# A whole transformer layer on one core: tiles with written places, new step tables for its first half, and a last product in two halves

## The chip, the cores and the metric

The kernel runs on one core of a Trainium2 chip. Its engines are TensorE (PE, which multiplies matrices), VectorE (DVE), ScalarE (ACT), GpSimd (POOL), and SyncE (SP), whose queue issues most transfers. The metric is the device time of one execution in microseconds, the median of several runs; less is better.

## The reference

One layer of a diffusion backbone is computed in float32, for 128 context tokens and 128 latent tokens of 2048 channels, with the same weights for both groups:

```python
m = silu(c) @ w_ada + b_ada                       # shift1, scale1, gate1, shift2, scale2, gate2
h = rms_norm(x) * (1 + scale1) + shift1
p = h @ w_in                                      # [q_A k_A v_A | q_B k_B v_B | gate_A gate_B]
o_A = windowed attention(q_A, k_A, v_A)           # 8 heads of 128, 2 key heads
o_B = neighbourhood attention(q_B, k_B, v_B)      # 8 heads of 128
merged = (sigmoid(gate_A) * (o_A @ w_br_a) + sigmoid(gate_B) * (o_B @ w_br_b)) @ w_out
x = x + gate1 * merged
h2 = rms_norm(x) * (1 + scale2) + shift2
y = x + gate2 * (relu(h2 @ w_up) ** 2 @ w_down)   # 2048 -> 8192 -> 2048
```

The new keys and values of both mixers are outputs too.

## The kernel before, in words

**Products.** Each float32 operand is split in two parts of a shorter form: `hi` is a copy in the shorter type, `lo` is the value less `hi`. A product is then three matmuls: hi by hi, hi by lo, lo by hi. The tokens stand in two blocks of 128 (context and latent), and the weights stream through as the moving operand.

**Steps.** All weight products are a list of steps, `wsteps`. One step is one weight tile `raw` of 128 rows by 1024 values (512 KB): two slices of 512 columns, two token blocks, three matmuls each, so twelve matmuls of 512 columns into two PSUM banks `acc`. The tile is loaded by SP's queue, copied to `wH` by ACT (line 103), and subtracted to `wL` by DVE (line 281). For the steps in `LO_DMA`, the low half is made by an accumulating transfer that POOL issues (lines 287 and 288) and DVE does nothing.

**What sets the order.** The order is written out; the engines each follow their own queue in that order. `run()` (line 305) goes through the steps. Ahead of a step's products it issues all loads up to `RUN[i]` steps ahead and prepares the tiles up to `LOOK[i] + 1` steps ahead; behind the products it runs what the calendar `cal[i]` holds for that step, entered there with `at(i, fn)`. So the strings `RUN` and `LOOK` and lists of step numbers (`DOTS`, `POST`, `JOBS`, `ADA_AT`, `XS_AT`, `SS_AT`) fix where each piece of small work stands in each engine's queue. A step of products that no one holds up takes 2.72 us, twelve times 0.227.

**Buffers.** All large tiles (`raw`, `wH`, `wL`, `araw`, `u_...`, `xnT` and so on) come from `G()`, which takes the next of 50 places of 4 KB per partition in rotation, the pool `gen`.

**The opening and the first 224 steps.** `begin()` (line 575 on) writes the steps 0 to 2 out by hand. The input projection follows in five chunks of channels (2, 2, 2, 4 and 6 tiles of 128). Each chunk needs its modulated input, for which the modulation (shift and scale) of two channel tiles at a time is made by `mod_pair(f)` (line 540): eight loads `araw` of 512 KB, sixteen column-tiled matmuls (line 366, 32 rows of the trace) into one bank `ps_ada`, a copy `S` by ACT, four transposes by PE into `ps_sel` (line 380), a sum by DVE, then the modulated and split input. `ADA_AT[f]` is the step at which it stands, and the transposes stand one step later. `SS_AT` does the same for the second sub-layer in two halves of eight matmuls. A unit of the projection that continues a sum from an earlier chunk either seeds its banks with ACT copies (`SEED1` has a 1) or adds by DVE behind its products (a 0, line 476).

The gates of the residuals are computed on DVE as dot products (line 1499, two instructions of 128 by 1024 each), placed by `DOTS`. The attention stands in steps 80 to 130: norms and rotation (`POST`), and for eight jobs of heads the scores (line 861), softmax, transposes to `ps_PT` (line 911), their copy `probT` by ACT, and the weighted values (lines 918 and 922), placed by `JOBS`. After it come the two branch products, the output product, the up and the down products.

**The ending.** `last_unit` (line 1216) does the last 512 output columns. The last two weight tiles' products for the latent tokens come last; then DVE multiplies by the gate and adds (lines 1067 and 1069) in two halves of 256 columns, each followed by its store (line 1411).

## Time and profile before

| | before |
|---|---|
| time, median of 3 runs (us) | 1313.86 (1313.8 to 1314.27) |
| time of the profiled execution (us) | 1313.68 |
| its span, first to last instruction (us) | 1311.8 |
| PE busy (us, share) | 1298.4, 99% |
| DVE busy | 1146.1, 87% |
| ACT busy | 917.5, 70% |
| POOL busy | 58.5, 4% |
| granted clock of TensorE, mean | 1.00 |
| HBM read, written (MB) | 373.97, 8.70 |

The span is less than the time by 1.9 us, which lie around the first and last instruction. A row of the timeline begins with the start and the duration in microseconds; in brackets behind it stands how long the engine had idled before and on what. Matmuls overlap: two neighbours start 0.227 us apart, though each is shown with 0.39 us, so waits of PE are read from the distances of starts.

### The profile page before, as it was taken

The page shows a single profiled execution, that of the slowest core. Times are in us where ns is not written, and L with a number is a line of the kernel's source. Part 1 is how long each engine was busy: PE and PEld are TensorE (multiplying, and loading weights), DVE is VectorE, ACT ScalarE, POOL GpSimd, SP SyncE. Part 2 cuts the span into 40 slices and gives each one's busy share as a digit, 9 for nine tenths or more (in the row PEclk, how much of TensorE's full clock was granted, in tenths as well). Part 3 has the DMA queues.
Part 4 walks back from the last instruction along what each step waited for, and adds up shares of the span by engine and source line. Part 5 has one row for each costly group of instructions (what it writes and reads, how often), then busy time and mean ns, then how long its engine had stood idle before and what let it go on. Part 6 is the DMA issues. An engine that isn't in the chain of part 4 may idle for free.

```text
span 1311.8 us, 17435 instructions
## 1 busy us (share of the span) xinstructions
PE 1298.4 (99%) x5978; PEld 1052.2 (80%) x5978; DVE 1146.1 (87%) x1532; ACT 917.5 (70%) x1289; POOL 58.5 (4%) x67
## 2 busy tenths in 40 slices
PE   8999999999999999999999999999999999999998
PEld 4767888888777778888888888888888888888886
DVE  4578999999899999999879998897989999979653
ACT  5657766689765657645687857869678787796881
POOL 0000000341100000000000000000000000000000
PEclk9999999999999999999999999999999999999999
DMA  9999998897889999999399775788586696968692
GB/s 379 418 411 420 361 365 320 306 364 278 290 347 365 419 384 330 369 344 372 113 321 317 244 256 179 273 293 282 201 297 224 212 317 248 297 161 304 204 345 78
DMA packets 148313, 393.80 MB, mean 300 GB/s; under 512 B 51680, under 2 KB 52672, under 8 KB 148224
## 3 DMA queue, kind: packets, MB, share of 16 engines
q1 hardware_dynamic: 144064, 378.18, 77.7%
q0 software_dynamic: 4016, 14.42, 5.7%
q8 instruction: 47, 0.77, 0.2%
q14 instruction: 42, 0.34, 0.1%
q10 hardware_dynamic: 144, 0.08, 0.0%
HBM read 373.97 MB, written 8.70 MB: 292 GB/s over the span
## 4 chain that ended last, share of the span: by engine, by line
PE 70%; DVE 3%; ACT 0%; issue 0%; DVEq 0%; ACTq 0%
PE acc L332 14%; PE acc L333 14%; PE acc L334 14%; PE Q L1281 6%; PE Q L1283 6%; PE Q L1282 6%; PE Z L1281 1%; PE Z L1283 1%; PE Z L1282 1%; DVE aT L1499 1%; DVE junk L1499 1%; PE acc L1119 1%; PE acc L1120 1%; PE acc L1102 1%; PE acc L1101 1%; PE acc L1103 1%
## 5 line engine op out<-in xcount | busy, mean ns | idle before, releaser
L281 DVE TENSOR_TENSOR wL<-raw,wH 128x1024 fp32r<-128x1024 f32 x361 | 425.7, 1224 | 62.4 <-ACT wH L103 61.8
L103 ACT ACTIVATE wH<-raw 128x1024 fp32r<-128x1024 f32 (+1 forms) x391 | 387.4, 1043 | 49.7 <-PE acc L334 10.2
L1499 DVE SCALAR_TENSOR_TENSOR aT<-aT,cB 128x1024 f32<-128x1024 f32 x144 | 173.9, 1224 | 1.1
L1499 DVE SCALAR_TENSOR_TENSOR junk<-aT,cB 128x1024 bf16<-128x1024 f32 x144 | 173.9, 1224 | 0.0
L463 PE MATMUL acc<-wH,hH 128*128 128x512 f32 x276 | 108.2, 392 | 0.0
L465 PE MATMUL acc<-wH,hL 128*128 128x512 f32 x276 | 107.5, 389 | 0.0
L464 PE MATMUL acc<-wL,hH 128*128 128x512 f32 x276 | 107.5, 389 | 0.0
L103 ACT ACTIVATE uH<-raw 128x1024 fp32r<-128x1024 f32 x34 | 36.1, 1063 | 65.7 <-DVE raw L1345 57.9
L463 PEld LDWEIGHTS acc<-wH,hH 128*128 128x128 f32 x276 | 51.8, 188 | 13.8 <-issue 2.5
L465 PEld LDWEIGHTS acc<-wH,hL 128*128 128x128 f32 x276 | 51.8, 188 | 10.9
L464 PEld LDWEIGHTS acc<-wL,hH 128*128 128x128 f32 x276 | 51.8, 188 | 10.6
L103 ACT ACTIVATE tH<-t 128x1024 fp32r<-128x1024 f32 x34 | 36.0, 1058 | 28.7 <-DVE t L1338 26.5
L332 PE MATMUL acc<-wH,hH 128*128 128x512 f32 x128 | 52.6, 411 | 0.0
L333 PE MATMUL acc<-wL,hH 128*128 128x512 f32 x128 | 50.1, 392 | 1.3 <-DVE wL L281 1.3
L498 PE MATMUL acc<-wH,hH 128*128 128x512 f32 x128 | 50.5, 394 | 0.0
L499 PE MATMUL acc<-wL,hH 128*128 128x512 f32 x128 | 49.9, 390 | 0.1
L334 PE MATMUL acc<-wH,hL 128*128 128x512 f32 x128 | 50.1, 391 | 0.0
L500 PE MATMUL acc<-wH,hL 128*128 128x512 f32 x128 | 50.0, 390 | 0.0
L1348 DVE TENSOR_TENSOR uL<-raw,uH 128x1024 fp32r<-128x1024 f32 x34 | 41.7, 1226 | 1.4 <-ACT uH L103 0.3
L103 ACT ACTIVATE acc<-dsum 128x512 f32<-128x512 f32 x56 | 31.7, 590 | 15.7 <-DVE t L1067 8.3
L1338 DVE TENSOR_TENSOR t<-raw 128x1024 f32<-128x1024 f32 x34 | 41.4, 1219 | 1.3 <-PE Q L1282 1.3
L1347 DVE TENSOR_TENSOR tL<-t,tH 128x1024 fp32r<-128x1024 f32 x34 | 41.4, 1219 | 0.0
(652 smaller groups left out, 3331.9 us busy)
## 6 DMA issues: line engine op xcount, KB each, us to landing
raw<-in_w_in SPq DMA_DIRECT2D x133, 512.0 KB, 7.6
raw<-in_w_down SPq DMA_DIRECT2D x128, 512.0 KB, 6.3
aT<-in_w_adaT SPq DMA_DIRECT2D x80, 512.0 KB, 8.0
raw<-in_w_upF SPq DMA_DIRECT2D x68, 512.0 KB, 5.4
aT<-in_w_gT SPq DMA_DIRECT2D x64, 512.0 KB, 7.7
raw<-in_w_up SPq DMA_DIRECT2D x60, 512.0 KB, 6.2
araw<-in_w_pair SPq DMA_DIRECT2D x48, 512.0 KB, 8.9
raw<-in_w_out SPq DMA_DIRECT2D x32, 512.0 KB, 9.2
```

The source lines that it names most:

```text
L103: act.activation(out, in_, AF.Copy)
L281: dve.tensor_tensor(st["lo"], st["raw"], st["hi"].bitcast(F32), op=OP.subtract)
L332: pe.matmul(acc[tb], sh, wh[:, k, :], start=f, stop=False, skip_group_check=seeded)
L333: pe.matmul(acc[tb], sh, wl[:, k, :], start=False, stop=False, skip_group_check=seeded)
L334: pe.matmul(acc[tb], sl, wh[:, k, :], start=False, stop=l, skip_group_check=seeded)
L463: pe.matmul(acc[tb], sh, wh[:, k, :], start=opened[u] and k == 0, stop=False, skip_group_check=skip)
L464: pe.matmul(acc[tb], sh, wl[:, k, :], start=False, stop=False, skip_group_check=skip)
L465: pe.matmul(acc[tb], sl, wh[:, k, :], start=False, stop=last and k == 1, skip_group_check=skip)
L1281: pe.matmul(acc, stat[0], hi, start=f, stop=False)
L1282: pe.matmul(acc, stat[0], lo, start=False, stop=False)
L1283: pe.matmul(acc, stat[1], hi, start=False, stop=l)
L1499: dve.scalar_tensor_tensor(out, box["raw"], 1.0, cB[s, tag], op0=OP.mult, op1=OP.mult, accum_out=dst[:, s, fb:fb + 1])
```

## The change

**Places written down.** `G()` no longer rotates. A string `SLOTS` gives for every tile, in the order in which they are asked for, the letter of one of 53 places, each a buffer of its own. Three more tiles are 12 KB more per partition; the program is built with a space of 4096 bytes for DMA descriptors (`SCRATCH`), which it did not set before.

**New tables.** For the first 224 steps `LOOK`, `RUN` (digits now to base 36, the largest 14 where it was 9), `LO_DMA`, `DOTS1`, `DOTS`, `SEED1` (25 ones where there were 27), `POST`, `JOBS`, `XS_AT` and `M_AT` are other numbers; `DOTS2` and the digits of the later steps stay.

**The modulation in four pieces.** `wide_load` and `wide_mm` now handle two `araw` tiles (four matmuls) at a time, and `ADA[f]` gives for each of the four pieces the step of its loads and of its products, then the steps of the transposes, of the input and of its split. `SS` does so for the second sub-layer.

**Warm-up.** The tile `wr`, its two copies by ACT, and the six matmuls on it in `begin()` are replaced by six matmuls of the other warm-up form.

**The ending.** The last 24 products become 48 of 256 columns by the words of the change; in the program built from it, twelve matmuls of 512 columns become twenty-four of 256 (each with its weight load), first all of the left half, then the DVE work of that half, then the right half.

```diff
@@ -28,13 +28,15 @@
-GEN = 50
+SLOTS = 'ABCDEFGHIJKLMNOPQRSTUVWXYZabcdefghijklmnopqrstuvwxyz0GHIJKLMNERSTUOPhdQiVekjWXYaZbmlpocuvsrwyzTSAPOx0IWjJKYXNZ...
+GEN = 53
+SCRATCH = 4096
...
-SEED1 = "111110100100111111011111111001011111"
+SEED1 = "010010101101111110101110011111111110"
...
-LO_DMA = [50, 54, 56, 63, 77, 107, 129, 144, 145, 176, 184, 188, 189, 203, 228, 233, 250, 286, 297, 360, 388, 392, 403, 447]
+LO_DMA = [50, 54, 57, 63, 77, 107, 118, 126, 132, 142, 144, 184, 188, 189, 203, 233, 250, 286, 297, 360, 388, 392, 403, 447]
...
-ADA_AT = [None, 4, 13, 22, 25]
-XS_AT = {1: 3, 2: 24, 3: 34}
...
-JOBS = [[93, 94, 95, 100, 106], [93, 94, 99, 104, 106], [98, 98, 100, 105, 114], [101, 104, 107, 110, 111], [107, 107, 110, 115, 118], [109, 109, 111, 118, 121], [113, 114, 115, 126, 128], [116, 116, 119, 122, 124]]
-SS_AT = [118, 127]
+ADA = {1: [[1, 2, 3, 5], [0, 2, 4, 5], [5, 5, 5]], 2: [[13, 14, 15, 18], [11, 14, 16, 17], [18, 19, 20]], 3: [[17, 18, 18, 22], [17, 18, 21, 21], [21, 21, 27]], 4: [[24, 26, 26, 26], [25, 27, 27, 27], [28, 29, 30]]}
+XS_AT = {1: 1, 2: 19, 3: 20}
...
+JOBS = [[92, 94, 99, 102, 106], [94, 95, 100, 104, 106], [98, 99, 100, 106, 114], [103, 104, 108, 110, 111], [107, 107, 110, 114, 119], [108, 109, 111, 119, 122], [114, 114, 115, 123, 126], [114, 116, 119, 123, 124]]
+SS = [[[117, 119, 122, 126], [116, 119, 125, 127], 129]]
...
@@ -90,8 +92,13 @@
+    slots = iter(SLOTS)
+
+    def slot():
+        return {"tag": "g" + next(slots), "bufs": 1} if SLOTS else {"tag": "g"}
+
     def G(name, dt=F32):
-        return gp.tile([P, 1024], dt, name=name, tag="g")
+        return gp.tile([P, 1024], dt, name=name, **slot())
...
-    wr = G("wr", F32R)
...
-    for h in range(2):
-        copy(wr[:, 512 * h:512 * h + 512], wm)
...
-    def wide_load(box, nsub, f, half):
-
-        for q in range(4 * half, 4 * half + 4):
+    def wide_load(box, nsub, f, j):
+
+        for q in (2 * j, 2 * j + 1):
...
     def mod_pair(f):
 
         box, k0 = {}, 2 * f
-        i = ADA_AT[f]
-        for j in range(2):
-            load_at(i, lambda j=j: wide_load(box, 0, f, j))
-            at(i, lambda j=j: wide_mm(box, j))
-        at(i, lambda: ada_evac(box))
-        at(i + 1, lambda: ada_cols(box, 0, k0, 2))
-        at(i + 2, lambda: make_h(k0, 2))
-        at(i + 3, lambda: split_h(k0, 2))
+        come, go, (c, m, s) = ADA[f]
+        for j in range(4):
+            load_at(come[j], lambda j=j: wide_load(box, 0, f, j))
+            at(go[j], lambda j=j: wide_mm(box, j))
+        at(go[3], lambda: ada_evac(box))
+        at(c, lambda: ada_cols(box, 0, k0, 2))
+        at(m, lambda: make_h(k0, 2))
+        at(s, lambda: split_h(k0, 2))
...
-        warm_r(*[(P, wr[:, 0:512])] * 3, *[(P, wr[:, 8:520])] * 3)
+        warm(6)
...
-        def mms(q, tb):
+        def mms(q, tb, c=slice(0, 512)):
             wh, wl = box["hl"][q]
+            acc = box["acc"][tb][:, c]
             for k in range(2):
                 sh, sl = stat(q // 2)(2 * (q % 2) + k, tb)
...
+                pe.matmul(acc, sh, wh[:, k, c], start=False, stop=False, skip_group_check=True)
+                pe.matmul(acc, sh, wl[:, k, c], start=False, stop=False, skip_group_check=True)
+                pe.matmul(acc, sl, wh[:, k, c], start=False, stop=q == n - 1 and k == 1, skip_group_check=True)
...
                     evac_s(box["acc"], 0)
-                    mms(q - 1, 1)
-                    mms(q, 1)
                     for c in (slice(0, 256), slice(256, 512)):
+                        mms(q - 1, 1, c)
+                        mms(q, 1, c)
                         evac_s(box["acc"], 1, c)
...
-    nc = bacc.Bacc("TRN2", target_bir_lowering=False, num_devices=1)
+    nc = bacc.Bacc("TRN2", target_bir_lowering=False, num_devices=1, dynamic_dma_scratch_size=SCRATCH)
```

On SP, behind the opening, where the first pair's modulation is loaded (`raw` are weight tiles, `araw` the modulation's), before:

```order
L255 DMA raw_182<-in_w_in 128x1024 [waits DMAHW3_49]
L255 DMA raw_184<-in_w_in 128x1024 [waits DMAHW4_49]
L255 DMA raw_186<-in_w_in 128x1024 [waits DMAHW5_49]
L255 DMA raw_188<-in_w_in 128x1024 [waits DMAHW6_49]
L196 DMA silu_151<-srow_224 32x128 [waits DMAHW7_49,Activation_49]
L255 DMA raw_366<-in_w_in 128x1024 [waits DMAHW0_49]
L356 DMA araw_372<-in_w_pair2 128x1024 [waits DMAHW1_49]
L356 DMA araw_374<-in_w_pair2 128x1024 [waits DMAHW2_49]
L356 DMA araw_376<-in_w_pair2 128x1024 [waits DMAHW3_49]
```

and of the change:

```order
L253 DMA raw_179<-in_w_in 128x1024 [waits DMAHW3_49]
L253 DMA raw_181<-in_w_in 128x1024 [waits DMAHW4_49]
L354 DMA araw_183<-in_w_pair2 128x1024 [waits DMAHW5_49]
L354 DMA araw_185<-in_w_pair2 128x1024 [waits DMAHW6_49]
L253 DMA raw_187<-in_w_in 128x1024 [waits DMAHW7_49]
L354 DMA araw_189<-in_w_pair2 128x1024 [waits DMAHW0_49]
L354 DMA araw_191<-in_w_pair2 128x1024 [waits DMAHW1_49]
L253 DMA raw_193<-in_w_in 128x1024 [waits DMAHW2_49]
L194 DMA silu_148<-srow_229 32x128 [waits DMAHW3_49,Activation_49]
L354 DMA araw_371<-in_w_pair2 128x1024 [waits DMAHW4_49]
```

The first four modulation tiles have moved ahead: two stand in front of the third weight tile, two in front of the fourth, and the rest comes two by two behind that.

On PE, where the transposes `ps_sel` of the first pair's modulation stand, before:

```order
L464 MATMUL acc_465<-wL_357,hH0_248 128x512
L465 MATMUL acc_465<-wH_355,hL0_249 128x512
L380 MATMUL ps_sel_481<-ident_93,S_454 128x128 [waits Activation_49]
L380 MATMUL ps_sel_481<-ident_93,S_454 128x128 x3
L463 MATMUL acc_491<-wH_368,hH0_248 128x512
L464 MATMUL acc_491<-wL_370,hH0_248 128x512 [waits DVE_49]
```

and of the change:

```order
L364 MATMUL ps_ada_401<-araw_379,rt_90 32x512 [waits DMAHW0_49]
L364 MATMUL ps_ada_401<-araw_379,rt_90 32x512
L364 MATMUL ps_ada_401<-araw_381,rt_90 32x512 [waits DMAHW1_49]
L364 MATMUL ps_ada_401<-araw_381,rt_90 32x512
L378 MATMUL ps_sel_482<-ident_92,S_480 128x128 [waits Activation_49]
L378 MATMUL ps_sel_482<-ident_92,S_480 128x128 x3
L461 MATMUL acc_498<-wH_430,hH0_253 128x512
```

Before, the transposes stand between products, twelve of them behind the last modulation matmul; now they follow the last piece's matmuls at once, and ACT's copy `S` of that same bank is what they wait for.

On PE at the very end, before (`acc_11557` is the latent tokens' bank):

```order
L1225 MATMUL acc_11557<-wL_11582,a15H_11336 128x512
L1226 MATMUL acc_11557<-wH_11580,a15L_11337 128x512
L1224 MATMUL acc_11557<-wH_11580,a15H_11336 128x512
L1225 MATMUL acc_11557<-wL_11582,a15H_11336 128x512
L1226 MATMUL acc_11557<-wH_11580,a15L_11337 128x512
```

and of the change, around the place where the left half ends and the right half begins:

```order
L1225 MATMUL acc_11548<-wH_11571,a15L_11328 128x256
L1223 MATMUL acc_11548<-wH_11571,a15H_11327 128x256
L1224 MATMUL acc_11548<-wL_11573,a15H_11327 128x256
L1225 MATMUL acc_11548<-wH_11571,a15L_11328 128x256
L1223 MATMUL acc_11548<-wH_11567,a15H_11327 128x256 [waits DVE_49]
L1224 MATMUL acc_11548<-wL_11569,a15H_11327 128x256
L1225 MATMUL acc_11548<-wH_11567,a15L_11328 128x256
```

The products have half the columns and twice the number, and the right half's first one waits for a DVE instruction, the multiplication that reads the left half of the same bank; the program before has no wait among its last twelve.

## What was predicted

> **What bounds the kernel now.** I read the busy line of the page first, then windows of 20 us, then the timeline of TensorE (PE) in each window with idle time. The columns of a window are its stretch, its length, then busy time and number of instructions of PE, weight load, VectorE (DVE), ScalarE (ACT), GpSimd, then the granted clock, the DMA share and GB/s.
>
> ```profile
> PE 1298.4 (99%) x5978; PEld 1052.2 (80%) x5978; DVE 1146.1 (87%) x1532; ACT 917.5 (70%) x1289; POOL 58.5 (4%) x67
> 60.00:80.00 20.00, 19.87 (x105) 13.81 (x104) 11.05 (x19) 12.72 (x20) 0.00 (x0) 1.00 1.03 417
> 320.00:340.00 20.00, 19.10 (x103) 15.80 (x101) 19.83 (x37) 19.22 (x65) 6.23 (x6) 1.00 0.84 284
> 400.00:420.00 20.00, 19.24 (x106) 16.25 (x105) 20.00 (x33) 12.49 (x18) 0.86 (x1) 1.00 0.98 353
> ```
>
> PE is busy 1298.4 of 1311.8 us and the clock is full, so a schedule can win only what is left in PE's pauses: 13.4 us, a good part of it in the opening and the ending. The tables that change govern the first 224 steps. The pauses there that I can name are these (start, duration, and in brackets the idle time with its releaser):
>
> ```profile
> 75.80 0.39 PE L498 MATMUL acc<-wH,hH 128*128 128x512 f32 x1
> 76.32 0.50 PE L499 MATMUL acc<-wL,hH 128*128 128x512 f32 x1
> 334.41 0.48 PE L332 MATMUL acc<-wH,hH 128*128 128x512 f32 x1
> 335.45 0.50 PE L333 MATMUL acc<-wL,hH 128*128 128x512 f32 x1 [0.56 <-DVE wL L281]
> 367.11 0.39 PE L334 MATMUL acc<-wH,hL 128*128 128x512 f32 x1
> 368.72 0.70 PE L918 MATMUL ps_o<-probT,u_kvA 128*128 128x512 f32 x1 [1.22 <-ACT probT L103]
> 413.92 0.39 PE L332 MATMUL acc<-wH,hH 128*128 128x512 f32 x1
> 415.07 0.50 PE L333 MATMUL acc<-wL,hH 128*128 128x512 f32 x1 [0.76 <-DVE wL L281]
> 473.43 0.27 PE L1520 MATMUL ps_gr<-ident,gc_g 128*32 128x128 f32 x1 [0.82 <-DVE gc_g L1505]
> ```
>
> Products of 512 columns normally start 0.227 us apart (1306.41 and 1306.64 in the last fence below). By starts, the low half wL comes late by 76.32 - 75.80 - 0.227 = 0.3 us, by 0.8 and by 0.9, with some 0.1 more each on the next interval: 2.3 us in three places. The softmax weights probT come late by 1.61 - 0.227 = 1.4 us. The gate rows gc_g come late by 0.8. Added to them is the opening's modulation load:
>
> ```profile
> 29.51 0.39 PE L463 MATMUL acc<-wH,hH 128*128 128x512 f32 x1
> 35.04 3.45 PE L366 MATMUL ps_ada<-araw,rt 128*32 128x512 f32 x24
> 38.68 1.05 PE L366 MATMUL ps_ada<-araw,rt 128*32 128x512 f32 x4 [0.19 <-DMA araw<-in_w_pair]
> 39.98 1.05 PE L366 MATMUL ps_ada<-araw,rt 128*32 128x512 f32 x4 [0.25 <-DMA araw<-in_w_pair]
> 40.97 0.50 PE L463 MATMUL acc<-wH,hH 128*128 128x512 f32 x1
> 41.08 0.60 ACT L103 ACTIVATE S<-ps_ada 128x512 f32<-128x512 f32 x1 [5.33 <-PE ps_ada L366]
> 41.58 2.00 ACT L103 ACTIVATE wH<-raw 128x1024 fp32r<-128x1024 f32 x2
> DMA packets 3467, 11.69 MB, mean 417 GB/s; under 512 B 398, under 2 KB 430, under 8 KB 3466
> ```
>
> The last line is the DMA view of 20 to 48 us: 0.524 MB at 417 GB/s is 1.26 us per tile, and the last two of the eight modulation tiles reach PE 1.30 us apart. From 35.04 to 40.97 PE needs 5.9 us for a block that elsewhere takes 3.6 (next fence): it waits 2.3 us.
>
> **The wide pieces.** The modulation's blocks of column-tiled products are cut in four and laid between ordinary products. By PE's order 6 blocks become 15 (some pieces stand together). What does another block cost?
>
> ```profile
> 65.84 0.39 PE L465 MATMUL acc<-wH,hL 128*128 128x512 f32 x1
> 66.16 3.64 PE L366 MATMUL ps_ada<-araw,rt 128*32 128x512 f32 x32
> 69.73 0.50 PE L463 MATMUL acc<-wH,hH 128*128 128x512 f32 x1
> 70.07 0.40 PE L464 MATMUL acc<-wL,hH 128*128 128x512 f32 x1
> 393.51 0.39 PE L334 MATMUL acc<-wH,hL 128*128 128x512 f32 x1
> 393.83 1.92 PE L366 MATMUL ps_ada<-araw,rt 128*32 128x512 f32 x16
> 395.68 1.05 PE L922 MATMUL ps_o<-probT,u_vB 128*128 128x128 f32 x7
> ```
>
> A whole block of 32 records takes 69.73 - 65.84 - 0.227 = 3.66 us, a half of 16 takes 395.68 - 393.51 - 0.227 = 1.94. Two halves are 0.22 dearer than one whole, and the return costs 70.07 - 69.73 - 0.227 = 0.11 more: 0.33 us a block. Nine more are **+3.0**. Nothing hides this: it is PE's own time. The attention's short groups (scores, transposes, values) stand side by side more often, about seven returns fewer at 0.08 each (rows in the last fence: 353.95 - 353.64 - 0.227): **-0.6**. The bounds are +2.0 to +3.0; I take +2.4.
>
> **The first block's wait.** In the new order of SP's queue the first two pieces' tiles come after raw tiles 3 and 4, the second pair behind raw 5; before, all eight came behind raw 7. With tile eight at 39.95 and 1.26 a tile, the slots are 24.9, 26.2, 27.4, 28.7, 29.9, 31.2, 32.4. PE reaches the pieces at 29.51. The first two tiles are there (27.4, 28.7) and take 0.9; tile three comes at 31.2 and tile four at 32.4: waits of 0.75 + 0.85 = 1.6 us for 2.3 before: **-0.7**. The later pieces' tiles land at least 1.5 us ahead. If PE waited for nothing it would be -2.3.
>
> **Transposes that follow their copy at once.** For pairs 1 and 3 the four transposes of S now stand right behind the last piece on PE; before, a step of twelve products lay between. ACT started the copy 0.11 after PE's next product (41.08 against 40.97) and took 0.60; with the hand-off PE stands 0.75 us: twice, **+1.5**. ACT had idled 5.33 us before that copy, so I take it as prompt; behind two copies of wH it would be 2.0 us more each.
>
> **The stalls the tables move.** The first three (wL) lie in places where DVE's queue runs short. Added over its rows, DVE has by the products of the second stall 9.9 us less work ahead than before, for the dot products of the gate vectors are placed earlier, into the first 100 us, where DVE is busy 11.05 of 20. I take them away: **-2.3**; kept, 0. Two more units than before begin without a seed, which costs DVE four additions:
>
> ```profile
> L476 DVE TENSOR_TENSOR u_qA<-u_qA,acc 128x512 f32<-128x512 f32 x4 | 2.7, 688 | 4.1 <-PE acc L465 4.0
> L1499 DVE SCALAR_TENSOR_TENSOR aT<-aT,cB 128x1024 f32<-128x1024 f32 x144 | 173.9, 1224 | 1.1
> L281 DVE TENSOR_TENSOR wL<-raw,wH 128x1024 fp32r<-128x1024 f32 x361 | 425.7, 1224 | 62.4 <-ACT wH L103 61.8
> ```
>
> That is 4 x 0.69 = 2.8 us, in the second chunk, under cover of the same idle time; without cover it is +2.8. The row of L1499 is one half of a dot product, that of L281 the subtraction that makes a wL. Between job 5's scores and its weighted values lie 24 products now and 12 before, 2.7 us for a stall of 1.4: **-1.4**. The chain to gc_g keeps its shape: 0. The warm-up products and the copies that fed them lie ahead of a wait for hH: 0. The new places and the smaller descriptor space move no instruction by themselves: 0, and a load that waited for its place would cost PE what it is late.
>
> **The ending.** The last twelve products become 24 of 256 columns. The rows are those of the scores, 128 columns each, and of the kernel's last microseconds:
>
> ```profile
> L861 PEld LDWEIGHTS ps_S<-T_kB,T_qB x32: 186/192/192, 352.7 to 387.8; 128*128 128x128 f32 x32
> 352.72 1.16 PE L861 MATMUL ps_S<-T_kB,T_qB 128*128 128x128 f32 x8
> 353.64 0.47 PE L332 MATMUL acc<-wH,hH 128*128 128x512 f32 x1
> 353.95 0.39 PE L333 MATMUL acc<-wL,hH 128*128 128x512 f32 x1
> 1305.07 0.69 DVE L1069 TENSOR_TENSOR x1b<-x1b,t 128x512 f32<-128x512 f32 x1
> 1306.41 0.39 PE L1225 MATMUL acc<-wL,a15H 128*128 128x512 f32 x1
> 1306.64 0.39 PE L1226 MATMUL acc<-wH,a15L 128*128 128x512 f32 x1
> 1307.06 0.42 DVE L1067 TENSOR_TENSOR t<-g,acc 128x256 f32<-128x256 f32 x1 [1.30 <-PE acc L1226]
> 1308.31 0.42 DVE L1069 TENSOR_TENSOR x1b<-x1b,t 128x256 f32<-128x256 f32 x1
> ```
>
> Eight of 128 columns need 0.92 us, 0.115 each, although a load takes 192 ns; half of 0.227 is 0.113, so I take 0.115. The left half starts at 1306.64 - 11 x 0.227 = 1304.14 and ends 11 x 0.115 + 0.28 later, at 1305.7. DVE's addition runs to 1305.76; then it multiplies the left half, 0.42, to 1306.2. But in PE's order the right half's first product waits for this multiplication, for both halves lie in one bank. It starts at 1306.25 and the twelve end at 1307.8; multiplication and addition with hand-offs, 0.92, end at 1308.7. Before, the last addition ended at 1308.31 + 0.42 = 1308.73. **0**, though the first half's output leaves earlier. Without that wait the products would end at 1307.04: -0.8.
>
> [...]
>
> **The sum.** +2.4 - 0.7 + 1.5 - 2.3 - 1.4 + 0 = -0.5 us against the profiled execution's 1313.68, which is the span of 1311.8 and 1.9 around it. That gives 1313.2; the median of the runs, 1313.86, lies 0.2 above that execution. I predict **1313.1**. Its own range takes the bounds one at a time: 1311.5 with no wait for the first block or with both copies hidden, 1315.4 with the three stalls kept, 1317.1 with both copies of S behind copies of wH; so 1311.3 to 1316.
>
> **The rivals.** A change below 0.2% (2.63 us) can't be told from none.
>
> *The schedule wins more.* ACT's copy of S and the early tiles come in time and the wait for gc_g goes too: -1.5 - 1.6 - 0.8 further, 1309.2. For it: ACT idles before the copies. Against it: the order on PE puts nothing between the last piece and the transposes, and the tile slots are full (417 GB/s). It need hold only in part: 1311. Chance 0.35 that the time is below 1311.2.
>
> *DVE becomes late elsewhere: slower.* In 400 to 420 us DVE is busy all 20.00 us, in 320 to 340 19.83. Each wL takes its 1.22 us in one queue with the dot products (2 x 1.22 each). A dot placed one step too early there stops PE for about 1 us, as at 334 and 413. Should the three stalls stay (+2.3) and two more arise from the four additions, whose cover has gone by then (2 x 1.0), it is 1317.5. It decides from the point where a subtraction starts later than 1.3 us before its product. For it: stretches with no idle time. Against it: 9.9 us less work ahead. Chance 0.15.
>
> *The loads of the 256-column products stand in line:* 24 x (0.19 + 0.115) in place of 24 x 0.115; with the wait between the halves the ending is about 4 us longer: 1317. The row of L861 speaks against it: loads of 192 ns, products 0.115 apart. [...] Chance 0.02, within the slower ones' 0.15.
>
> *The table does not do what it says:* if places written down make a load wait for its place, SP's queue stands behind it and raw tiles come late; a load that comes a step later than it is needed costs PE that step, 12 x 0.227 = 2.7 us, 1315.8. Against it: the new run-ahead digits reach up to 14 steps where the old ones reach 9. It too is in the 0.15.
>
> **The numbers.** The forecast has 0.50, the better schedule 0.35, the slower ones 0.15. Leaving out about 0.2 at both ends: 1309.4 to 1316.9.
>
> **What would show it.** In the new profile: 15 blocks of column-tiled products with 0.33 us lost at each; two waits of about 0.75 for S before the transposes; waits for araw of 1.6 near 30 us; no wait for wL near the old places and none for probT; in the ending a pause of PE of about 0.5 us between the halves. I am wrong if waits for wL appear at new places, if PE waits for raw, or if the blocks cost no switch.

## The result, and the profile after

The changed kernel takes **1328.76 us** (median of 4 runs, 1326.66 to 1332.3) where the kernel before takes 1313.83 beside it (1313.61 to 1314.27): the ratio is **1.0115**, 95% interval 1.0102 to 1.0127. It is 15 us slower, above the predicted range. The four runs differ with the mean granted clock of TensorE: 1326.66 us at 0.999, 1328.5 and 1329.03 at 0.997, 1332.3 at 0.996. The profiled execution took 1329.03 us with a span of 1327.2. Line numbers of the changed kernel are one or two smaller than those of before around the products (L463 is now L461, L1282 is L1281), and the general copy of ACT, L103 before, is L110.

From the page of the changed kernel, the busy time of each engine:

```profile
PE 1307.5 (99%) x5990; PEld 1052.6 (79%) x5990; DVE 1150.2 (87%) x1538; ACT 911.2 (69%) x1275; POOL 60.1 (5%) x67
```

The work is nearly as before: DVE's 1150.2 us against 1146.1 are six more additions of 0.68 us behind units without a seed, 16 for 10. PE has 9.1 us more of busy time, part of which is the same products at half the clock, as will be seen, and its pauses grew from 13.4 to 19.7. The view of PE's waits in the changed kernel (line that waited, what released it: total us, times, longest):

```profile
PE Q L1280 <- ACT up L1186: 2.7, 2, 2.5
PE ps_sel L378 <- ACT S L110: 2.1, 3, 0.7
PE ps_gr L1519 <- DVE gc_g L1504: 1.7, 1, 1.7
...
PE ps_qT L812 <- DVE u_kvA L789: 1.2, 1, 1.2
...
PE Q L1281 <- DMA XL<-in_w_upF: 1.0, 1, 1.0
PE ps_qT L812 <- DVE u_kvA L799: 0.9, 1, 0.9
PE acc L496 <- DVE u_kB L474: 0.9, 1, 0.9
PE ps_ada L364 <- DMA araw<-in_w_pair: 0.7, 2, 0.6
```

The old waits are gone: none for wL, and none of the weighted values for probT. In their place stand waits for S, which the prediction has, and for u_kvA, u_kB, XL and the up product, which it has not. To see where the time comes from, I took the start of the same product in both traces and followed the difference, the **lag**:

| product of step | before (us) | after (us) | lag | since the row above |
|---|---|---|---|---|
| 29 | 120.22 | 125.67 | 5.45 | +5.45 |
| 90 | 286.50 | 296.29 | 9.79 | +4.34 |
| 130 | 437.09 | 443.94 | 6.84 | -2.95 |
| 199 | 628.54 | 637.38 | 8.84 | +2.0 |
| 218 | 682.26 | 697.30 | 15.04 | +6.2 |
| the last | | | 15.21 | +0.2 |

The places behind these steps, in PE's timeline of the changed kernel (start, duration; in brackets the idle time and its releaser):

```profile
45.04 0.65 PE L378 MATMUL ps_sel<-ident,S 128*128 128x128 f32 x4 [0.74 <-ACT S L110]
...
76.99 0.50 PE L496 MATMUL acc<-wH,hH 128*128 128x512 f32 x1 [0.87 <-DVE u_kB L474]
...
290.41 0.41 PE L812 MATMUL ps_qT<-ident,u_kvA 128*128 128x128 f32 x2 [1.24 <-DVE u_kvA L789]
291.73 0.41 PE L812 MATMUL ps_qT<-ident,u_kvA 128*128 128x128 f32 x2 [0.91 <-DVE u_kvA L799]
...
481.30 0.27 PE L1519 MATMUL ps_gr<-ident,gc_g 128*32 128x128 f32 x1 [1.71 <-DVE gc_g L1504]
...
687.03 0.50 PE L1281 MATMUL Q<-XL,h20H 128*128 128x512 f32 x1 [0.99 <-DMA XL<-in_w_upF]
688.07 0.40 PE L1282 MATMUL Q<-YB,h20L 128*128 128x512 f32 x1
691.00 0.51 PE L1280 MATMUL Q<-tH,sH 128*128 128x512 f32 x1 [2.54 <-ACT up L1186]
...
1321.46 0.38 PE L1223 MATMUL acc<-wH,a15H 128*128 128x256 f32 x1 [0.51 <-DVE t L1065]
1321.68 0.28 PE L1224 MATMUL acc<-wL,a15H 128*128 128x256 f32 x1
```

**Opening, to step 29, +5.45.** Seven more blocks of wide products at 0.34 are 2.4; the two waits for S cost 0.7 each beyond that (45.04); the first block waits 1.99 us over its streaming time where it was 2.35; the wait for u_kB at 76.99 costs 1.03. That is 4.5; the last 1.0 is spread over short waits that I did not settle. **Step 90, +4.34.** The transposes of the first key tile u_kvA wait twice (290.41, 291.73: 1.4 and 1.0 by starts), and the half clock behind them costs 1.6. **Steps 90 to 130, -2.95.** The stalls for wL and probT that stood here are gone, two more blocks are there. **To step 199, +2.0**, 0.9 of it the longer wait for gc_g. **Steps 217 and 218, +6.2.** PE waits 1.1 for XL (the product ahead of it starts at 685.66), 2.7 and 0.3 for ACT's copy `up`, and loses 1.7 to the half clock behind that.

The half clock, in windows of 1 us of the changed kernel (stretch, length, busy time of PE, weight load, DVE, ACT, POOL, then the granted clock, DMA share, GB/s):

```profile
293.00:294.00 1.00, 1.00 (x4) 0.81 (x3) 1.00 (x2) 0.69 (x3) 0.00 (x0) 0.50 1.06 418
693.00:694.00 1.00, 1.00 (x4) 0.74 (x3) 0.18 (x1) 0.78 (x1) 0.00 (x0) 0.50 0.00 0
```

Why is ACT late with `up`? It stands behind a copy of a transfer that came late. The timelines of ACT and of SP's queue, changed kernel:

```profile
686.86 2.51 ACT L110 ACTIVATE fTa<-pTa 128x2048 uint16<-128x2048 uint16 x1 [6.35 <-DMA pTa<-pla]
690.37 0.58 ACT L1186 ACTIVATE up<-acc 128x512 f32<-128x512 f32 x1
...
667.21 0.33 SPq L1485 DMA_DIRECT2D aT<-in_w_gT  x1
670.97 11.30 SPq L985 DMA_TRANSPOSE pTa<-pla  x1
682.32 1.05 SPq L1194 DMA_DIRECT2D x1d<-x  x2
```

and of SP's queue before:

```profile
660.47 2.51 SPq L987 DMA_TRANSPOSE pTa<-pla  x1
```

`pTa` is a transposing transfer (`flip`): its issue held SP's queue for 11.30 us where it held it for 2.51, and ACT had idled 6.35 us for it. New digits of `RUN` put more loads ahead of it.

### The profile page after: what moved, and what is told of

It reads as the page before. It is cut to its first block, busy times and chain, and to the rows that moved or that the text cites. A ratio compares the mean times of both kernels' runs of the same rounds, so it can differ in the third digit from the quotient of the medians.

```text
span 1327.2 us, 17405 instructions
## 1 busy us (share of the span) xinstructions
PE 1307.5 (99%) x5990; PEld 1052.6 (79%) x5990; DVE 1150.2 (87%) x1538; ACT 911.2 (69%) x1275; POOL 60.1 (5%) x67
## 4 chain that ended last, share of the span: by engine, by line
PE 67%; DMA 7%; DVE 4%; issue 1%; ACT 1%; SPq 0%; DVEq 0%; ACTq 0%
PE acc L330 12%; PE acc L331 12%; PE acc L332 12%; PE Q L1280 6%; PE Q L1281 6%; PE Q L1282 6%; DMA aT<-in_w_adaT 3%; DVE wL L279 2%; DMA raw<-in_w_br_a 1%; DMA pTa<-pla 1%; PE acc L498 1%; PE acc L497 1%; PE acc L496 1%; PE ps_S L859 1%; DVE junk L1498 1%
## 5 line engine op out<-in xcount | busy, mean ns | idle before, releaser
L110 ACT ACTIVATE wH<-raw 128x1024 fp32r<-128x1024 f32 (+1 forms) x391 | 385.2, 1042 | 26.9 <-PE acc L332 6.5
L461 PE MATMUL acc<-wH,hH 128*128 128x512 f32 x276 | 108.7, 394 | 0.1
L463 PE MATMUL acc<-wH,hL 128*128 128x512 f32 x276 | 107.5, 390 | 0.0
L110 ACT ACTIVATE uH<-raw 128x1024 fp32r<-128x1024 f32 x34 | 36.1, 1063 | 66.0 <-DVE raw L1344 64.0
L461 PEld LDWEIGHTS acc<-wH,hH 128*128 128x128 f32 x276 | 51.8, 188 | 16.6 <-ACT wH L110 1.7
L463 PEld LDWEIGHTS acc<-wH,hL 128*128 128x128 f32 x276 | 51.8, 188 | 10.9
L110 ACT ACTIVATE tH<-t 128x1024 fp32r<-128x1024 f32 x34 | 36.0, 1059 | 29.5 <-DVE t L1337 26.7
L110 ACT ACTIVATE fTa<-pTa 128x2048 uint16<-128x2048 uint16 x16 | 40.4, 2528 | 6.4 <-DMA pTa<-pla 6.4
L110 ACT ACTIVATE acc<-dsum 128x512 f32<-128x512 f32 x56 | 31.7, 591 | 15.6 <-DVE t L1065 8.3
```

Source lines behind the costliest of these rows:

```text
L110: act.activation(out, in_, AF.Copy)
L461: pe.matmul(acc[tb], sh, wh[:, k, :], start=opened[u] and k == 0, stop=False, skip_group_check=skip)
L463: pe.matmul(acc[tb], sl, wh[:, k, :], start=False, stop=last and k == 1, skip_group_check=skip)
```

## The experiments

All kernels below compute everything the reference asks for; one (the pauses) adds work. "Step" and "lag" are as above, and each ratio is to the kernel before, which ran beside each. Where the text says "by starts", it is the distance of two starts less the usual 0.227.

### The loads ahead of the transposing transfer, taken out of the change

`RUN[208]` to `RUN[210]` get the digits of before; each tile keeps its written place, so `SLOTS` is reordered to match. With the digits alone the program deadlocks: once places are written down, the order of the loads and the order of the places have to be changed together.

```diff
-RUN = "...6dcb5205a6cad5663..."
+RUN = "...6dcb5205538ad5663..."
```

> The changed kernel with three digits of the load table as before (steps 208, 209 and 210: 5, 3 and 8 steps ahead in place of 10, 6 and 12), so that the loads of steps 219 to 222, the two cB and the aT stand behind the first transposing transfer pTa on SP's queue and not ahead of it; each tile keeps its written place. Theory (a transposing transfer is held on SP until all of SP's earlier transfers have landed): its issue takes some 2.5 to 5 us in place of 11.3, PE's waits for XL (1.2 us) and for the bank that ACT frees late (2.7 us) go, and with them the stretch of half clock behind (2.0 us): 1322.8 us, 6 less than the changed kernel's 1328.76. Rival (the smaller descriptor space or the written places slow the transfers): issue stays near 11 us, time within 1 us of 1328.8.

Measured 1322.15 us (1321.48 to 1322.68), ratio 1.0062 (1.0047 to 1.0077): 6.6 us less than the change. SP's queue:

```profile
670.78 1.61 SPq L985 DMA_TRANSPOSE pTa<-pla  x1
```

The issue takes 1.61 us, the waits for XL and `up` and the half clock near 690 are gone, and the lag at the end is 8.75. That is as expected (1322.8).

### The same loads, put into the kernel before

```diff
-RUN = "...8511453877787785..."
+RUN = "...85114a6c77787785..."
-            while loads and loads[0][0] <= st["i"] + int(RUN[st["i"]]):
+            while loads and loads[0][0] <= st["i"] + int(RUN[st["i"]], 36):
```

> The kernel before with three digits of its load table as in the change (steps 208, 209 and 210: 10, 6 and 12 steps ahead in place of 5, 3 and 8), nothing else. Theory (the transposing transfer waits for all of SP's earlier loads): the first pTa is issued later or held for some 8 to 11 us (2.5 before), PE waits behind it as in the changed kernel: 1317 to 1320 us. Rival (the loads ahead of the transfer do not matter; places or descriptor space do): 1313.9 us.

Measured 1321.23 us (1321.05 to 1322.34), ratio 1.0057 (1.0042 to 1.0072): three digits alone cost the kernel before 7.4 us. SP's queue and PE's timeline in it:

```profile
664.45 12.40 SPq L987 DMA_TRANSPOSE pTa<-pla  x1
...
683.99 0.79 PE L1281 MATMUL Q<-tH,sH 128*128 128x512 f32 x1 [5.34 <-ACT up L1188]
```

PE stands for 5.34 us, and behind that the granted clock is 0.50 or 0.51 in every window of 1 us from 684 to 688. The time is a little above the 1317 to 1320 expected, and both directions agree: this part of the change is settled, at 6.6 to 7.4 us.

### The key transposes two steps later

```diff
-POST = {('kvA', 0): [81, 86, 88], ...
+POST = {('kvA', 0): [81, 86, 90], ...
```

> The changed kernel with the transposes of kvA at step 90 in place of 88 (before: 89), the rest of its normalisation where the change put it. Theory (DVE finishes kvA late, since its part now stands at step 86 and not 83): the waits of PE at 288.8 and 290.6 us (1.4 and 1.0 us) go and so does the stretch of half clock from 292.9 to 296.3 (1.6 us): 1324.8 us. Rival (DVE is behind as a whole): the wait only moves two steps on, to other products, 1328 us.

Measured 1326.79 us (1322.68 to 1328.15), ratio 1.009 (1.0071 to 1.0109). The waits at 290 and the half clock went, and the lag at step 90 fell from 9.79 to 5.40; but PE then waited 2.4 us at 309.40 for T_qA, ACT's copy of the transposed queries, and at step 96 the lag is 8.07 where the change has 9.42. So most of it came back, but not all; the new wait had no half clock behind it. What this leaves out is the direct test: the rotation itself at step 83 again and the transposes at 88. The changed kernel loads the constants that this work reads only at step 86 (`CONST_AT`; the kernel before at 83), so that edit alone is not possible, and it was not measured in another form.

### One step between S's copy and its transposes

```diff
-ADA = {1: [..., [5, 5, 5]], ... 3: [..., [21, 21, 27]], ...
+ADA = {1: [..., [6, 6, 6]], ... 3: [..., [22, 22, 27]], ...
```

> The changed kernel with the four transposes of S, the modulated input and (for the first pair) its split one step later for pairs 1 and 3, so that a step of twelve products stands between the last modulation piece and the transposes. Theory (PE waits for ACT's copy of S, 0.9 us at 43.7 and 0.9 us at 100.3): 1327.0 us, and in the trace both intervals from the last piece to the transposes fall from 1.3 us to about 0.4. Rival (the later input makes the next chunk's split late): the time stays at 1328.8 and a wait for hH appears.

Measured 1327.72 us (1323.61 to 1328.03), ratio 1.0095 (1.0078 to 1.0112). The two waits for S are gone, but now PE waits for the split weights:

```profile
51.09 0.49 PE L461 MATMUL acc<-wH,hH 128*128 128x512 f32 x1 [0.43 <-ACT wH L110]
52.35 0.50 PE L462 MATMUL acc<-wL,hH 128*128 128x512 f32 x1 [0.77 <-DVE wL L279]
...
108.63 0.50 PE L461 MATMUL acc<-wH,hH 128*128 128x512 f32 x1 [0.61 <-ACT acc L110]
```

and, in the last row, for a bank that ACT seeds (0.8 by starts). The lag at step 29 is 6.68 where it was 5.45. The rival holds in that other work comes late; the wait for hH that it named did not appear. The two waits for u_kvA are in this kernel too (1.4 and 1.0 us), but no half clock stands behind them; the last section sets the two kernels side by side.

### All three together

```diff
-RUN = "...6dcb5205a6cad5663..."
+RUN = "...6dcb5205538ad5663..."
-POST = {('kvA', 0): [81, 86, 88], ...
+POST = {('kvA', 0): [81, 86, 90], ...
-ADA = {1: [..., [5, 5, 5]], ... 3: [..., [21, 21, 27]], ...
+ADA = {1: [..., [6, 6, 6]], ... 3: [..., [22, 22, 27]], ...
```

> Three edits of the changed kernel together: loads behind the transposing transfer, transposes of kvA at step 90, transposes of S a step later for pairs 1 and 3. The last of them alone has been seen to bring about 1 us of the 1.8 it should. If the causes are separate the savings add: 6 + 4 + 1 = 11, 1317.8 us. Rival (what one frees the next eats, since DVE or the load stream is the bound): more than 1321 us. In both cases it does not come under the kernel before (1313.8), for switches of the pieces, a late addition at 75.7 us (1.0) and the gate rows (0.9) stay.

Measured 1324.03 us (1323.14 to 1324.06), ratio 1.0075 (1.006 to 1.009): no better than the loads alone. The savings do not add; the rival holds. Here the wait near 309 (2.4 us) has half clock behind it; the mean clock of the run is 0.998.

### Loads and key transposes one step later; then a seed, then a transfer

The next three start from the loads put right and the transposes at step 89.

```diff
-POST = {('kvA', 0): [81, 86, 88], ...
+POST = {('kvA', 0): [81, 86, 89], ...
```

> The changed kernel with the loads behind the transposing transfer (1322.15 measured alone) and the transposes of kvA at step 89, as before the change, in place of 88. At 90 the wait and the half clock went and 2.4 us came back at 309 us, for qA's transposes share step 90. Theory (at 89 DVE has ended kvA and the order of the other transposes stays): the waits at 288 to 292 (2.35) and the half clock behind them (1.3 to 1.6) go, 1318.3 us. Rival (DVE and ACT are behind there by what PE gains): 2 us or more of it come back as waits before 320 us, 1320.5 us.

Measured 1323 us (1321.42 to 1324), ratio 1.0069 (1.0057 to 1.0082). Against the kernel with the loads alone, the lag is 4.0 less at step 90 and 0.4 more at step 96: it all came back, which is more than the rival expected (1320.5), in one wait and half clock behind it, in PE's timeline of this kernel:

```profile
311.94 0.65 PE L859 MATMUL ps_S<-T_kvA,T_qA 128*128 128x128 f32 x2 [2.31 <-ACT T_qA L818]
```

Then the first nine digits of `SEED1` as before, so that the first units get seeds again:

```diff
-SEED1 = "010010101101..."
+SEED1 = "111110100101..."
```

> The same with the seeds of the second chunk as before the change (first nine digits 111110100 in place of 010010101), so that the unit whose bank PE wants at 75.7 us is freed by ACT's copy and not by DVE's two additions behind four subtractions. Theory (the addition is late by what stands ahead of it on DVE): PE's wait for u_kB (1.0 us) goes: 1.0 us less than the run without it. Rival (DVE's four additions less are free, and ACT's seeds cost as much elsewhere in the opening): no difference.

Measured 1323.8 us (1322.1 to 1324.33), ratio 1.0074 (1.0061 to 1.0086). The wait for u_kB shrank only to about 0.8, and a wait of 1.29 for ACT's seed u_qB came at 70.28. The run does not test the theory recorded for it. The edit takes away the additions of u_kvA and u_qB, for which PE had not waited (at 61.68 and 65.63 in the change, with idle time of DVE ahead of them), and adds two of u_qA. The two additions of u_kB, for which it waits, stand in every kernel: at 72.11 before, at 76.25 in the change, and at 77.28 here, behind four subtractions that start at 72.74.

Or step 92's low half by transfer, so that DVE has one subtraction less just ahead of the queries' work:

```diff
-LO_DMA = [50, 54, 57, 63, 77, 107, ...
+LO_DMA = [50, 54, 57, 63, 77, 92, 107, ...
```

> The run with the loads behind the transposing transfer and kvA's transposes at step 89 (1323.0), and the low half of step 92 made by transfer in place of DVE's subtraction. Theory (DVE has no idle time from 120 to 310 us, so PE's wait at 309 us for T_qA, behind DVE's and ACT's work, is DVE's lateness): the wait of 2.4 us shrinks by the 1.2 us taken, and the half clock behind it (1.3) may go with it: 1320.6 to 1321.8 us. Rival (ACT's copy is late by ACT's own order): 2.4 us stay, 1323 us.

Measured 1324.14 us (1322.84 to 1325.26), ratio 1.0077 (1.0063 to 1.0091). In PE's timeline:

```profile
291.82 0.50 PE L496 MATMUL acc<-wH,hH 128*128 128x512 f32 x1 [2.75 <-ACT acc L110]
...
314.55 0.49 PE L859 MATMUL ps_S<-T_kvA,T_qA 128*128 128x128 f32 x2 [0.47 <-ACT T_qA L818]
```

and in ACT's:

```profile
288.19 1.06 ACT L110 ACTIVATE wH<-raw 128x1024 fp32r<-128x1024 f32 x1 [8.60 <-DMA raw<-in_w_in]
```

The wait for T_qA shrank from 2.31 to 0.47. That does not show that DVE's queue sets it: PE came there 4.45 us later (lag 9.83 at step 92 against 5.38), and T_qA itself was later than in the run without this edit (the wait ends at 314.55, there at 311.94). PE was late because of the new wait of 2.75. The copy to wH for the transfer is prepared earlier, so ACT stood idle for 8.60 us until its raw tile had landed, and the copy that seeds PE's bank (291.19) stood behind it.

### Slack that the kernel before may have

The rival "the schedule wins more" asks whether the old stalls can be had for nothing. In the kernel before, the weighted values of job 3 one step later:

```diff
-JOBS = [..., [101, 104, 107, 110, 111], ...
+JOBS = [..., [101, 104, 107, 110, 112], ...
```

> The kernel before with one number changed: the weighted values of the fourth attention job a step later (112 in place of 111). Theory (the probT wait is a wait of its own; in the run with more low halves by transfer it went, and other waits came from those): PE's wait for probT at 367 us (1.4 us) goes and nothing comes in its place, 1312.5 us. Rival (DVE, fully busy there, is the bound): waits for wL of the same size appear within the next ten steps, 1313.9 us.

Measured 1314.47 us (1314.28 to 1314.83), ratio 1.0005 (0.9996 to 1.0014). The wait for probT is gone (lag -2.64 at step 112), and by step 115 the lag is +0.32:

```profile
377.33 0.50 PE L333 MATMUL acc<-wL,hH 128*128 128x512 f32 x1 [1.34 <-DVE wL L281]
```

The wait moved to the low half wL. Why it did, DVE's timeline shows: DVE itself stands idle for a copy `oHA` of the values that were put later, and behind that come half a dot product (1.22) and then the subtraction that PE waits for, from 376.06 on.

```profile
374.31 0.69 DVE L927 TENSOR_TENSOR oLA<-ps_o,oHA 128x512 fp32r<-128x512 f32 x1 [1.08 <-ACT oHA L103]
```

With two low halves more by transfer:

```diff
-LO_DMA = [50, 54, 56, 63, 77, 107, 129, ...
+LO_DMA = [50, 54, 56, 63, 77, 102, 107, 121, 129, ...
-JOBS = [..., [101, 104, 107, 110, 111], ...
+JOBS = [..., [101, 104, 107, 110, 112], ...
```

> The kernel before with the weighted values of the fourth attention job a step later (112 in place of 111) and two more low halves made by transfer (steps 102 and 121 in LO_DMA), which takes one subtraction of 1.22 us from DVE ahead of each of the two stalls at 334 and 414 us. Theory (these three stalls are separate): PE's waits for probT (1.4 us) and for wL (0.8 and 0.9 us) go, 1310.8 us. Rival (DVE's or ACT's queue is the bound and the waits move): 1313 to 1315 us.

Measured 1315.9 us (1315.43 to 1316.44), ratio 1.0015 (1.0007 to 1.0024): waits for wL of 1.6, 0.7 and 1.5 us came, one of them for a transfer that landed late, and the stall near 334 stayed (1.0). With four such transfers, 73, 88, 92 and 123:

```diff
-LO_DMA = [50, 54, 56, 63, 77, 107, 129, ...
+LO_DMA = [50, 54, 56, 63, 73, 77, 88, 92, 107, 123, 129, ...
```

> The kernel before with four more low halves made by transfer (steps 73, 88, 92 and 123, each prepared five to six steps ahead), nothing else. Theory (DVE is the bound from 120 to 620 us): 3.7 us less work on DVE ahead of the wait at 334 and one subtraction less ahead of that at 414, so the waits for wL (0.9 and 1.0 us) go: 1312.0 us. Rival (the transfers come late or crowd the loads, DMA being 0.91 busy there): waits for wL from DMA, or 1314 us and more.

Measured 1321.77 us (1320.95 to 1322.93), ratio 1.0059 (1.0046 to 1.0073). The wait near 334 is gone, but PE came there 10.2 us later, so the run does not show that the transfers took it away. In PE's timeline there is instead

```profile
291.24 0.79 PE L498 MATMUL acc<-wH,hH 128*128 128x512 f32 x1 [3.38 <-ACT acc L103]
```

and 1.8 us of the same kind at 244.72, with half clock behind them (2.4 and 1.6 us). In this stretch, 200 to 300 us, ACT stood idle for 14.1 us for raw tiles that had not landed, 1.6 before. These transfers and job 3's later values together:

```diff
-LO_DMA = [50, 54, 56, 63, 77, 107, 129, ...
+LO_DMA = [50, 54, 56, 63, 73, 77, 88, 92, 107, 123, 129, ...
-JOBS = [..., [101, 104, 107, 110, 111], ...
+JOBS = [..., [101, 104, 107, 110, 112], ...
```

> The same with the values of the fourth job at step 112. Alone that only moved its 1.4 us to a wait for wL at 375 us. Theory (that wait came back because DVE was full): with DVE's 3.7 us less it stays away, 1310.6 us, under the kernel before. Rival (it comes back by the order on DVE around steps 111 to 114, not by fullness): as without the later values.

Measured 1322.64 us (1322.43 to 1323.39), ratio 1.0066 (1.0054 to 1.0079); PE's product of wL still starts 1.54 us behind the one ahead of it (383.54 and 385.08). DVE was not full: it was busy 29.39 of the 34 us from 350 to 384. But at 382.06 it again stood idle 1.08 us for `oHA`, with the same half dot product and the subtraction behind it. So the rival of this run holds: the wait comes back by the order of DVE's queue, and not because the queue is full. None of the kernels tried beats the kernel before.

### The ending alone, and 53 places in rotation

The ending in halves, in the kernel before:

```diff
-                    mms(q - 1, 1)
-                    mms(q, 1)
                     for c in (slice(0, 256), slice(256, 512)):
+                        mms(q - 1, 1, c)
+                        mms(q, 1, c)
                         evac_s(box["acc"], 1, c)
```

> The kernel before with the ending of the change alone: the last twelve products as 24 of 256 columns, the left half and its multiplication first. Theory (the right half waits for the multiplication that reads the left half of the same bank, and the weight loads are hidden): a pause of about 0.5 us between the halves, products of 256 columns 0.113 to 0.118 apart, 0.0 to +0.2 us, 1313.9. Rivals: without the pause the halves would bring 0.8 us, 1313.1; loads in line would cost 4 us, 1318.

Measured 1314.17 us beside 1313.89, ratio 1.0002 (0.9993 to 1.0011). PE's and DVE's timelines:

```profile
1306.41 0.38 PE L1225 MATMUL acc<-wH,a15H 128*128 128x256 f32 x1 [0.51 <-DVE t L1067]
...
1308.60 0.42 DVE L1069 TENSOR_TENSOR x1b<-x1b,t 128x256 f32<-128x256 f32 x1
```

53 places in rotation and the smaller descriptor space:

```diff
-GEN = 50
+GEN = 53
-    nc = bacc.Bacc("TRN2", target_bir_lowering=False, num_devices=1)
+    nc = bacc.Bacc("TRN2", target_bir_lowering=False, num_devices=1, dynamic_dma_scratch_size=4096)
```

> The kernel before with 53 tiles in rotation and a descriptor space of 4096 bytes, nothing else. Theory (neither has a part in the loss): 1313.5 to 1314.5, and POOL's accumulating transfers land as before (7 to 10 us). Rival (the small descriptor space holds POOL's transfers up): more than 1316, with waits of PE for wL.

Measured 1314.71 us (1314.58 to 1314.95), ratio 1.0005 (0.9996 to 1.0015). Neither has a part in the 15 us that these runs could show (0.3 and 0.8 us). Written places without the new tables were not run; no wait of PE in the change names a raw tile, which is how a load that waits for its place would show.

### How long a pause costs clock

Twelve pauses of PE of six lengths are put between the steps 146 and 190 of the kernel before, each a chain of n small copies on ACT between two transposes.

```diff
+    def pause(n):
...
+        pe.transpose(ps[:, 0:P], ident, ident)
+        copy(IDLE[0], ps[:, 0:P])
+        for k in range(n):
+            copy(IDLE[(k + 1) % 2], IDLE[k % 2])
+        ps = bank("ps_idle")
+        pe.transpose(ps[:, 0:P], IDLE[n % 2], ident)
+    for i, n in zip(range(146, 192, 4), (2, 4, 6, 8, 10, 12, 2, 4, 6, 8, 10, 12)):
+        at(i, lambda n=n: pause(n))
```

> The kernel before with twelve forced pauses of PE, one every four steps from step 146 to 190: PE transposes a tile, ACT copies the result and then copies it on 2, 4, 6, 8, 10 or 12 more times (128 columns each), and PE waits for the last copy; the series stands twice. [...]

The whole took 1368.2 us. Start to start of the two transposes, and what the products behind lost (products 0.43 apart instead of 0.227):

| pause, start to start (us) | 1.32 | 2.0 | 2.7 to 2.8 | 3.37 | 4.05 | 4.73 |
|---|---|---|---|---|---|---|
| lost behind it, first (us) | 0 | 0 | 1.6 | 1.6 | 1.6 | 2.0 |
| lost behind it, second (us) | 0 | 0 | 1.3 | 1.6 | 1.6 | 1.6 |

The timeline of two pauses, 2.0 and 2.7, and the windows behind them:

```profile
497.23 0.27 PE L1598 MATMUL ps_idle<-ident 128*128 128x128 f32 x1
499.23 0.33 PE L1603 MATMUL ps_idle<-ident,idle 128*128 128x128 f32 x1 [1.73 <-ACT idle L103]
...
510.34 0.27 PE L1598 MATMUL ps_idle<-ident 128*128 128x128 f32 x1
513.03 0.33 PE L1603 MATMUL ps_idle<-ident,idle 128*128 128x128 f32 x1 [2.41 <-ACT idle L103]
```

```profile
499.30:503.30 4.00, 4.00 (x18) 3.30 (x19) 3.10 (x4) 4.00 (x5) 0.00 (x0) 1.00 1.01 413
513.10:516.50 3.40, 3.40 (x9) 2.71 (x10) 2.35 (x5) 3.40 (x4) 0.00 (x0) 0.52 0.98 400
```

After 2.0 us eighteen products fit in 4 us at full clock; after 2.7, nine in 3.4 us at half. So the pauses of 2.7 to 2.8 us cost 4.1 to 4.3 each, and those of 4.73 lost 2.0 and 1.6 us of clock behind them, hardly more than the 1.6 and 1.3 behind those. This kernel ran once.

## Why the prediction was wrong

**The switches, +2.4: right.** An ordinary block cost 0.34 (predicted 0.33), and nine more are 3.0; the smaller number allowed for fewer attention groups, which the lag doesn't show apart.

**The first block's wait, -0.7: mis-sized.** Measured -0.35: 1.99 us of wait by starts, where the sum had 1.6.

**Transposes behind the copy of S, +1.5: right,** 0.7 twice. What the step left out is that putting them later again costs more.

**The stalls moved, -2.3 and -1.4: they went, but for the reason given only in part.** The wait for probT is gone. The 24 and 12 products that were counted for it lie between job 5's scores and job 3's transposes; between these transposes and their values stand 12 in both kernels. Of the three stalls for wL, the first lies in the opening, and PE waits there for u_kB instead, 1.03 us. The second went as predicted: DVE starts that subtraction at 327.88, in the kernel before at 334.18. The third went by luck. DVE ends that subtraction at 419.66, later than before (415.02), and has slightly more work ahead of it; the stall is gone because PE comes 8 us later itself (421.97, before 413.92). **The step that failed is the reason, "DVE has by the products of the second stall 9.9 us less work ahead".** That sum is right for step 104; it was made at one old stall and taken for all steps. Added in the same way at the other steps, DVE's queue has 5.3 us *more* work ahead than before at step 90, 7.5 at 91, 10.2 at 94. There the rotation of u_kvA came late, and PE lost 2.4 us and 1.6 us of clock. DVE's timeline of the change shows the four subtractions ahead of the additions of the opening (which come up below), two new additions, and the rotation of u_kvA:

```profile
71.71 4.63 DVE L279 TENSOR_TENSOR wL<-raw,wH 128x1024 fp32r<-128x1024 f32 x4 [1.30 <-ACT wH L110]
76.25 1.28 DVE L474 TENSOR_TENSOR u_kB<-u_kB,acc 128x512 f32<-128x512 f32 x2
...
285.05 1.28 DVE L474 TENSOR_TENSOR u_vB<-u_vB,acc 128x512 f32<-128x512 f32 x2
...
289.51 0.41 DVE L787 TENSOR_TENSOR u_kvA<-u_kvA,rq 128x256 f32<-128x256 f32 x1
```

The rotation of before, at its place there:

```profile
273.06 0.42 DVE L789 TENSOR_TENSOR u_kvA<-u_kvA,rq 128x256 f32<-128x256 f32 x1
```

Before, it was done 11 us ahead of its transposes, at step 83; the new `POST` has it at step 86 and the transposes one step earlier, at 88. Between 285.05 and the rotation DVE has no idle time. That this order makes the rotation late is read from the timeline; that the waits and the half clock hang on it, the run with the transposes at 90 shows. The rival "DVE becomes late elsewhere" had this mechanism, with 0.15 and other places (wL), and too low a price, for it left out the clock.

**The four additions, covered: miscounted, and the price lay elsewhere.** There are six more. Those of the second chunk stood under idle time of DVE, and no wait of PE names them. The wait for u_kB (1.03 us at 76.99) hangs on two additions that the kernel before has as well, there behind 4.6 us of idle time. What is new is the four subtractions ahead of them (71.71 to 76.25), which no term has. No run took those subtractions away, so this cause is read from the timeline alone. u_vB's two additions at 285.05 have no cover: they stand ahead of the late rotation.

**The gc_g chain, 0: wrong by 0.9.** The chain has its old shape, but DVE reached it later: 2.09 us by starts where it was 1.21.

**SP's queue: not looked at where it mattered.** The rival about SP asked whether a load comes late, and took the longer run-ahead for a help. What came late was the transposing transfer that loads were put in front of, 6.6 us of the 15.2, or 43%. Its row in the view of SP's queue stood in the profile before; the sum has no term for it. This is the second step that failed, and the one best shown: both directions were run.

**The clock, in no step.** Two stretches at half clock (near 293 and 692) cost 1.6 and 1.7 us. The prediction read "the clock is full" as a constant; in the change it was 0.50 for 3.41 us behind each of two stretches of the same length in which PE had been idle for 1.8 and 2.3 us, as the last section shows. The signs of being wrong that it named (waits for wL at new places, waits for raw, blocks without a price) did not come at all: the loss lay where it had no sign.

**The ending and the places, 0: right.** The pause between the halves was 0.51, the products 0.12 apart (1321.68 and the next at 1321.80); the rival of loads that stand in line has fallen. **"The schedule wins more", 0.35: wrong.** The copy of S made PE wait as the sum had it, and gc_g took longer. Even in the kernel before, the removal of a wait brought nothing. How full the engines are is one part of it. One window of 220 us of each, before and after:

```profile
120.00:340.00 220.00, 219.03 (x1014) 181.95 (x1012) 215.60 (x328) 165.37 (x345) 38.53 (x34) 1.00 0.91 333
```

```profile
126.00:346.00 220.00, 217.85 (x995) 180.95 (x994) 215.30 (x331) 157.50 (x329) 39.93 (x34) 0.99 0.87 321
```

DVE is busy 98% of it (215.60 and 215.30 of 220), about as much as PE. That PE is 99% busy led me to call it the bound; DVE has hardly more room in this stretch. But that a full DVE brings the waits back is not shown, and one run speaks against it: with four low halves by transfer DVE is busy 205.1 of 220 us (129 to 349), and the wait that job 3's later values had removed came back all the same. What brings it back there is the order of DVE's queue, in which one idle wait of 1.08 us makes the subtraction behind it late. And work taken off DVE by a transfer asks ACT for its copies before the tiles have landed, so that ACT stands idle (8.60 us once, 14.1 us in another run) and seeds banks late.

Two small things in the sum: 1313.68 - 0.5 is 1313.2, or 1313.4 from the median, where 1313.1 was predicted; and the range "1311.3 to 1316" leaves out the bound of 1317.1 that stands beside it. Neither matters against 15 us.

What stays open: about 1.0 us of the opening and 0.3 near step 90 lie in short waits that were not separated. Between steps 130 and 199 another 1.1 came besides gc_g, of which four waits of 0.13 to 0.34 us make some 0.9; the longest is for a bank that DVE frees late, at step 164.

## What to carry to other kernels

Where two engines are nearly full, add up the work ahead of each wait at every step that the table touches, not only at the old stalls. A stall that disappears may only show that the work went elsewhere, or that the waiting engine itself now comes later. Find the transfers that hold their queue (a transposing one here, for 11.30 us) and count what a longer run-ahead puts in front of them. Look at the granted clock behind PE's waits, and not only at each wait by itself: in the change two waits of 1.4 and 1.0 us close together were paid again with 1.6 us of clock, as the forced pauses of 2.7 to 2.8 us were with 1.6 and 1.3.

## What the hardware showed

**The issue of the transposing transfer, with few and with more loads ahead of it.** With few loads in flight SP's issue of `pTa` lasted 1.61 and 2.51 us, with more 11.30 and 12.40. From the trace's records of landings: in the change the load `aT` ahead of it landed at 682.71, the issue ended at 682.27 and `pTa` landed at 686.78; before, the last earlier load landed at 663.07 and the issue ended at 662.98. The kernel before and the change have 19 such transfers each. In the 12 that were issued with three or more of SP's earlier transfers still under way, the issue lasted 2.51 to 11.30 us and ended 0.09 to 0.45 us before the last of these landed; in the 15 with none under way it took 1.3 to 3.0 us. What holds it, no run here tells. The page's part on DMA issues, over 655 to 690 us of the change, has the time from issue to landing:

```profile
pTa<-pla SPq DMA_TRANSPOSE x1, 15.8
```

With the loads moved back it was 3.7.

**Half the clock behind two waits, and none behind the same two.** In the change the granted clock was 0.50 twice, from 292.9 to 296.3 and from 692.3 to 695.7, and 1.00 in the stretches around them (6.3 to 292.9, 296.4 to 692.2, 695.8 to 1327.0). The 3.41 us ahead of the first of these, and two stretches of that length over the same waits in the kernel with S's transposes a step later:

```profile
289.52:292.93 3.41, 1.61 (x9) 1.25 (x10) 3.34 (x9) 3.00 (x6) 1.07 (x2) 1.00 1.04 423
```

```profile
288.16:291.57 3.41, 2.24 (x10) 1.50 (x8) 3.34 (x7) 3.41 (x6) 0.00 (x0) 1.00 1.03 422
291.57:294.98 3.41, 2.42 (x12) 1.93 (x13) 3.34 (x6) 2.88 (x7) 1.07 (x2) 1.00 1.03 413
```

In the change PE was idle for 1.8 us of the 3.41 ahead of the first half clock (the stretch less PE's busy time), and for 2.3 us of those ahead of the second, from 688.88 to 692.29 with 1.09 busy. In the other kernel the stretches over the two waits for u_kvA have 1.2 and 1.0 us idle, and no half clock follows. In the same way the wait of 2.4 us for T_qA near 309 had no slow product behind it with the transposes at step 90; that of 2.31 with the loads put right and the transposes at 89 had, and the granted clock is 0.94 there over 310 to 340 us. The forced pause of 2.0 us (PE idle for 1.73) had full clock behind it, that of 2.7 us (2.41) half. So the same waits of some 2 us cost clock in one kernel and none in another; what decides it, these runs do not show.
